# Nine more places for raw weights in the room of the attention pool, and fourth sums added by a transfer

## The chip, the core and the metric

The kernel runs on one core of one Trainium2 chip. The metric is the device time of one execution in microseconds (us). The core has five engines with instruction queues of their own: TensorE (PE, matmuls), VectorE (DVE), ScalarE (ACT), GpSimd (POOL) and SyncE (SP, which here only issues transfers). SP and POOL both issue DMA transfers, which run on the core's 16 DMA engines.

## What is computed

One decoder layer over 512 tokens of width 2048. The normalised input is multiplied by one wide weight matrix; eight heads of latent attention (MLA) and eight heads of forgetting attention (FoX) follow, each gated by a SiLU path, then one output projection, a norm and the residual sum.

```python
h = _rms_norm(x, g_pre)
proj = h @ w_in
(q_lat, kv_lat, k_rope_raw, gate_mla,
 fq, fk, fv, f_logit, gate_fox) = jnp.split(proj, split_points, axis=-1)
o_mla = _mla_branch(q_lat, kv_lat, k_rope_raw, g_q, w_uq, g_kv, w_ukv, cos, sin) * jax.nn.silu(gate_mla)
o_fox = _fox_branch(fq, fk, fv, f_logit, b_forget) * jax.nn.silu(gate_fox)
o = jnp.concatenate([o_mla, o_fox], axis=-1) @ w_out
return x + _rms_norm(o, g_post)
```

All inputs are float32. The kernel keeps that precision by writing every factor as a sum of a rounded high part and a remainder, and by three matmuls in place of one (`mm3`, lines 138 to 140: high x high, high x low, low x high).

## The kernel before, in words

**Chunks.** All weights come as chunks of 128 partitions x 1024 float32 (512 KB). `load` (lines 215 to 238) has SP fetch a chunk into a place of the tag "raw"; `divide` (240 to 251) has ScalarE cast it to its high part `whi` (L249) and VectorE subtract to get the low part `wlo` (L250). `chunk(i)` (line 260) is called when TensorE's program comes to chunk i: it loads up to chunk i+4, divides up to chunk i+2, and hands out the parts of chunk i. There are three raw places, three `whi` and three `wlo`, all in the pool `wp`. A place is free again when both parts of the chunk that had it are made, so SP, whose queue is in order, waits at a load until that place is free.

**Stages.** First the FoX heads in four pairs (projections fq, fk, fv, fg, interleaved with the attention of the pair before). Then the stage of the change, which runs from about 436 us to 603 us: two groups of columns of the input projection, "l" (the latents) and "m" (the MLA gates), each as a 2 x 2 block product done with seven half-block products in place of eight. Their names are p1, p2, p4, q6, g5, g7 and g3, each of four chunks. They run in the order p1 l, p1 m, p2 l, p2 m, p4 l, p4 m, then q6, g5, g7, g3 for l, and the same four for m. In the chunk numbers of the program, p1 l has raw73 to raw76, p1 m 77 to 80, p2 81 to 88, p4 l 89 to 92, p4 m 93 to 96, and q6 l begins with raw97. A last stage does the MLA heads (projections mq, mk, mv, interleaved with attention) and the output projection, which is made of half-block products too.

**Sums of weights.** Half-block products need sums of weight blocks. These are made ahead in DRAM, in steps (`add_step`, line 289): a plain copy of one block into a scratch tensor, and then an accumulating transfer from POOL that adds the second block. A step is issued after every so many half chunks (`set_pace`, `paced`), and begins with a 64-byte transfer from `whi` that ties it to TensorE's progress (the rows `t<-whi`). During the stage of the change the pace is 1000, so no step is issued; it is 2 during the MLA heads. The fourth sums (t4, used by p4) of l and m are left for late: p4's chunk is t6 loaded into a raw place, and a second block loaded beside it (`second`), which VectorE adds into the raw place (line 246) before the cast.

**Operands.** The sums of input blocks, which are the other factor, were put away in DRAM by POOL (`awaymg`), and are fetched back by SP in 256 KB pieces (`fetch`, line 908: bmq for q6, bmg for g5, g7 and g3) and divided by ScalarE and VectorE (lines 129 and 130). POOL puts away parts of the finished FoX heads in the first part of the stage in the same way (`awayoa`, `awayog`, line 884).

**Order.** Instructions of one engine run in the order of the program, which a scheduler sets from the order of the code and from its own estimates. Each transfer counts on one of eight counters of its queue in turn (DMAHW0 to 7 for SP, DMASW0 to 7 for POOL), and an issue waits for the one that had its counter before.

**Room.** The pool `pp` holds what the attention of the heads works with (probabilities, their parts, values). Before, it stays open from the start to the end of the heads, also during the stage of the change, in which it is not used.

Of the kernel before, what the change touches and what calls it, by code (L numbers as in the profile page):

```python
# [12 lines left out]
F32 = mybir.dt.float32  # L13
# [3 lines left out]
ALU = mybir.AluOpType  # L17
AX = mybir.AxisListType

P = 128  # L20
# [22 lines left out]
RND = 12582912.0  # L43
V3 = 3 * HW
NSLOT = 28


def split_const(c, bits, n):
# [15 lines left out]
def tile_hybrid_layer(  # L64
# [16 lines left out]
    nc = tc.nc  # L81
    pe, act, dve, pool = nc.tensor, nc.scalar, nc.vector, nc.gpsimd
# [4 lines left out]

    inner = ctx.enter_context(ExitStack())
    tb = inner.enter_context(tc.tile_pool(name="tb", bufs=1))
    pp = inner.enter_context(tc.tile_pool(name="pp", bufs=2))  # L90
    tp = inner.enter_context(tc.tile_pool(name="tp", bufs=4))
    dr = ctx.enter_context(tc.tile_pool(name="dr", bufs=1, space=bass.MemoryType.DRAM))
    ps = ctx.enter_context(tc.tile_pool(name="ps", bufs=4, space=bass.MemoryType.PSUM))

    def slot(name, dt=F32, shape=(P, 2, S)):

        return sp.tile(list(shape), dt, tag="s", name=name)
# [4 lines left out]
    def proj_bank(name):  # L102
        return bank("pj", name, 4)
# [90 lines left out]
    chunks = []  # L194
# [11 lines left out]

    raws, ready = {}, {}

    more = []

    def raw_tile(i):
        pool = more[0] if more and (i - more[1]) % 6 < 3 else wp
        return pool.tile([P, 1024], F32, tag="raw", name=f"raw{i}", bufs=3)

    def load(i, small=None):

        w, cols, k, n, width = chunks[i]
        if cols is None:

            raw = raw_tile(i)  # L220
            nc.sync.dma_start(raw, w)
            raws[i] = raw
            if k is not None:
                second = slot(f"second{i}")
                nc.sync.dma_start(second, k)
                raws[i] = raw, second.rearrange("p k c -> p (k c)")
            return
        if i < 2:
            raw = slot(f"raw{i}", shape=(P, 1024))
        else:  # L230
            raw = raw_tile(i)
        v = raw[:, : n * width].rearrange("p (k c) -> p k c", k=n)
        for at, off, cnt in cols:
            (nc.sync if cnt >= P or small is None else small).dma_start(
                v[:, :, at : at + cnt],
                w[0, k * P : (k + n) * P, off : off + cnt].rearrange("(k p) c -> p k c", p=P),
            )
        raws[i] = raw

    def divide(i):  # L240
        w, cols, k, n, width = chunks[i]
        m = n * width
        raw = raws.pop(i)
        if isinstance(raw, tuple):
            raw, second = raw
            dve.tensor_tensor(out=raw, in0=raw, in1=second, op=ALU.add)
        hi = wp.tile([P, 1024], F32R, tag="whi", name=f"whi{i}")
        lo = wp.tile([P, 1024], F32R, tag="wlo", name=f"wlo{i}")
        act.copy(hi[:, :m], raw[:, :m])  # L249
        dve.tensor_tensor(out=lo[:, :m], in0=raw[:, :m], in1=hi[:, :m].bitcast(F32), op=ALU.subtract)  # L250
        ready[i] = [t[:, :m].rearrange("p (k c) -> p k c", k=n) for t in (hi, lo)]
# [6 lines left out]
            state["divided"] += 1  # L258

    def chunk(i, ahead_load=4, ahead=2):  # L260
        while state["loaded"] < min(len(chunks), i + ahead_load + 1):
            load(state["loaded"])
            state["loaded"] += 1
        prepare(i + ahead)
        return ready.pop(i)

    fox = []
    for p in range(4):
        c = {}
# [45 lines left out]
    prods = {}  # L315
# [165 lines left out]
    def set_pace(n):  # L481
        state.update(pace=n, tiles=0)
# [435 lines left out]
    def along(a, b):  # L918
        return [lambda x=x, y=y: (x(), y()) for x, y in zip(a, b)]
# [4 lines left out]
    def operand(n, of):  # L924
        def parts(kk, t):
            return [oper[n, of][kk // 2][:, x, kk % 2, t * P : (t + 1) * P] for x in range(2)]

        return parts
# [126 lines left out]
    for p in range(4):  # L1055
        c = fox[p]
# [152 lines left out]
    def sums_wide(n):  # L1209
        return lambda kk: [oper[n, "m"][kk // 2][:, x, kk % 2, :] for x in range(2)]  # L1210
# [30 lines left out]
    def gate(f, top, bottom):  # L1241

        if f % 2 == 0:
            o_of.append(slot(f"gm{f // 2}"))
        g = o_of[-1][:, f % 2, :]
        pt = att_bank(f"gmt{f}")
        c = slice(f % 4 * P, (f % 4 + 1) * P)
        for t in range(NT):
            pe.transpose(pt[:, t * P : (t + 1) * P], (top, bottom)[t // 2][:, t % 2, c], ident)
        act.activation(g, pt, AF.Tanh)  # L1250
        dve.scalar_tensor_tensor(out=g, in0=g, scalar=1.0, in1=pt, op0=ALU.add, op1=ALU.mult)
        gm.append(g)

    set_pace(1000)
    A, A2 = ([proj_bank(f"g{n}{t}") for t in range(2)] for n in "lm")
    product("p1", "l", x_wide(0, 0), A, True, True, turned=True)
# [22 lines left out]
    scaled(c21, B2, 2, pb)  # L1279
    drain()  # L1280
    C, G = ([proj_bank(f"g{n}l{t}") for t in range(2)] for n in "cd")
    product("q6", "l", sums_wide("q6"), C, True, True, side=[*f5[2:], *along(d5[:2], f7[:2])], turned=True)
    raws_of += [slot(f"lat{i}") for i in (2, 3)]
    lat_sum(lat_block(1, 0), C, pl, ALU.subtract)
# [34 lines left out]
    drain()  # L1319
    for f in range(4, 8):  # L1320
        todo.append(lambda f=f: gate(f, c12, c22))
    qnh, qnl = zip(*(latents[i] for i in range(6)))
    knh, knl = zip(*(latents[i] for i in range(6, 10)))


    for p in range(4):
        c = mla[p]
        if p == 3:
            for f in (*fetches("a11", "o"), *fetches("a12", "o")):
                f()  # L1330
        qb = [proj_bank(f"mq{p}{i}") for i in range(3)]

        proj_T(c["q"], [(qb[i], P, cols(i * P)) for i in range(3)], qnh, qnl, rate=2)
        q = [[split(qb[i], f"mq{p}{i}", SC_M, first=P)] for i in range(2)]
        wholes = slot(f"mw{p}")
        qw = [[whole_block(wholes, i, qb[i], SC_M)] for i in range(2)]
        a, b = rotate(qb[2], P, SC_M, f"q{p}")
        for i in range(2):
            r = tmp(f"rq{p}{i}")
            src = slice(ROPE * i, ROPE * (i + 1))  # L1340
            for half in range(2):
                dve.tensor_tensor(
                    out=r[ROPE * half : ROPE * (half + 1), :], in0=a[src, :], in1=b[src, :], op=ALU.add
                )
            q[i].append(split(r, f"rq{p}{i}", first=P))
            qw[i].append(whole_block(wholes, 4 + i, r))
        if p == 0:
            set_pace(2)
        if p == 3:
            todo.extendleft([*divisions("a11", "o"), *divisions("a12", "o")])  # L1350
        kb = [proj_bank(f"mk{p}{i}") for i in range(2)]
        vb = [proj_bank(f"mv{p}{i}") for i in range(2)]

        def v_cols(w, j):
            return w[:, j, :].rearrange("p (h c) -> p h c", h=2)[:, :, NOPE:]

        kk = 0
        for i in c["kv"]:
            hi, lo = chunk(i)
            for j in range(chunks[i][3]):  # L1360
                fst, lst = kk == 0, kk == KVR // P - 1
                for n in range(2):
                    w = cols(256 * n)
                    mm3(kb[n], w(hi, j), w(lo, j), knh[kk], knl[kk], fst, lst)
                for t in range(NT):
                    o = vb[t // 2][:, (t % 2) * 256 : (t % 2) * 256 + 256]
                    ts = slice(t * P, (t + 1) * P)
                    mm3(
                        o, knh[kk][:, ts], knl[kk][:, ts], v_cols(hi, j), v_cols(lo, j),
                        fst and t % 2 == 0, lst, skip_group_check=True,  # L1370
                    )
                kk += 1
                pump(2)
                behind(hi)
        k = [[split(kb[i], f"mk{p}{i}"), (kr, None)] for i in range(2)]
        kw = [[whole_block(wholes, 2 + i, kb[i]), kr.bitcast(F32)[:, :P]] for i in range(2)]
        drain()
        values_into(v_pair(f"mv{p}"), slice(0, 256), [piece_of(vb, t, 256)[0] for t in range(NT)])
        vs = values_of(f"mv{p}")
        heads = [  # L1380
            Head(
                f"m{2 * p + i}", q[i], k[i],
                vs[i],
                lambda h=2 * p + i: gm[h],
                list(zip(qw[i], kw[i])),
            )
            for i in range(2)
        ]
        enqueue_scores(heads)
        enqueue_values(heads)  # L1390
        done += heads
# [124 lines left out]
            s()  # L1516

    product("p2", 0, operand("a12", "o"), A, False, True, 2, (6, heads_end))
    inner.close()
    op = ctx.enter_context(tc.tile_pool(name="op", bufs=8, reuse_waits="tile"))  # L1520
    more.extend([op, state["loaded"]])
# [9 lines left out]
    f = og_of[1, 0]  # L1531
# [78 lines left out]
```

## Time and profile before

| | before |
|---|---|
| median of three runs | 910.28 us (908.63 to 911.88) |
| the profiled execution | 912.14 us, span 910.4 us |
| TensorE busy | 898.7 us, 99% of the span |
| VectorE busy | 625.2 us, 69% |
| ScalarE busy | 424.6 us, 47% |
| granted TensorE clock | 0.997 of full speed |
| moved by DMA | 199.40 MB, mean 219 GB/s |

The span runs from the first to the last instruction; the rest of the execution lies around it. A row of the timeline gives the start, the duration, engine, line, operation, what is written and read, and in brackets the idle time of the engine just before with what ended it. A matmul's end is modelled, and matmuls overlap, so how long one step of TensorE takes is read from one start to the next. A row of the waits gives who waited for whom: us in total, times, the longest. A row of the windows gives the stretch, its length, the busy time of each engine with its number of instructions, the granted clock, the mean share of the DMA engines that were busy, and GB/s.

### The profile page before, as it was taken

To read this page: it belongs to the slowest core of one execution; us is meant where nothing else is said; L and a number is where in the kernel's file an instruction comes from. 1 tells how busy PE (TensorE), PEld (TensorE's weight loads), DVE (VectorE), ACT (ScalarE), POOL (GpSimd) and SP (SyncE) were. 2 spreads that over 40 slices of the span, in tenths; PEclk is the share of its full clock that TensorE was granted. 3 is DMA by queue.
4 is the path that set the end of the run, shared out by engine and by line. 5 is a ranking of instruction groups with operands and counts; after the bars stand their busy time and mean duration, and the time that the engine had idled before them with its cause. 6 is when DMAs were issued, how large, how long until landed. Compare 5 with 4: busy or idle time off the path is not lost.

```text
span 910.4 us, 12934 instructions
## 1 busy us (share of the span) xinstructions
PE 898.7 (99%) x4732; PEld 774.3 (85%) x4732; DVE 625.2 (69%) x1074; ACT 424.6 (47%) x779; POOL 80.9 (9%) x97
## 2 busy tenths in 40 slices
PE   8999999999999999999999999999999999999997
PEld 8988888898889988888998998878888888888885
DVE  3467778537563684474758777978877986886585
ACT  5773333234222342242464556644554565654483
POOL 1010110110120110111100000001101000000021
PEclk9999999999999999999999999999999999999998
DMA  9378987987898798899798875559999546786878
GB/s 291 96 197 192 250 218 199 231 222 195 231 256 210 200 233 226 228 219 228 228 312 304 289 221 162 162 157 230 215 231 254 117 122 203 243 257 216 278 188 251
DMA packets 121364, 199.40 MB, mean 219 GB/s; under 512 B 16050, under 2 KB 59596, under 8 KB 121300
## 3 DMA queue, kind: packets, MB, share of 16 engines
q1 hardware_dynamic: 105044, 158.84, 55.5%
q0 software_dynamic: 15520, 39.33, 23.5%
q8 instruction: 37, 0.61, 0.3%
q10 hardware_dynamic: 736, 0.40, 0.2%
q14 instruction: 27, 0.22, 0.1%
HBM read 186.46 MB, written 70.80 MB: 283 GB/s over the span
## 4 chain that ended last, share of the span: by engine, by line
PE 92%; DVE 4%; DMA 2%; ACT 1%; issue 1%; SPq 0%; ACTq 0%; DVEq 0%
PE fv L561 4%; PE fg L138 3%; PE fq L140 3%; PE fq L138 3%; PE fq L139 3%; PE fg L140 3%; PE fg L139 3%; PE fk L139 3%; PE fk L140 3%; PE fk L138 3%; PE sm L604 3%; PE fv L140 2%; PE fv L138 2%; PE fv L139 2%; PE mq L138 2%; PE mq L140 2%
## 5 line engine op out<-in xcount | busy, mean ns | idle before, releaser
L250 DVE TENSOR_TENSOR wlo<-raw,whi 128x1024 fp32r<-128x1024 f32 (+3 forms) x205 | 242.8, 1186 | 172.3 <-ACT whi L249 162.2
L249 ACT CAST whi<-raw 128x1024 fp32r<-128x1024 f32 (+3 forms) x205 | 209.4, 1022 | 297.5 <-PE fk L139 52.9
L138 PE MATMUL fq<-h,whi 128*128 128x512 f32 x128 | 52.6, 411 | 0.0
L138 PE MATMUL fg<-h,whi 128*128 128x512 f32 x128 | 51.0, 398 | 0.0
L140 PE MATMUL fq<-h,wlo 128*128 128x512 f32 x128 | 50.3, 393 | 0.0
L139 PE MATMUL fq<-h,whi 128*128 128x512 f32 x128 | 50.1, 391 | 0.0
L140 PE MATMUL fg<-h,wlo 128*128 128x512 f32 x128 | 50.1, 391 | 0.0
L138 PE MATMUL fk<-h,whi 128*128 128x512 f32 x128 | 50.0, 391 | 0.0
L139 PE MATMUL fg<-h,whi 128*128 128x512 f32 x128 | 49.9, 390 | 0.0
L139 PE MATMUL fk<-h,whi 128*128 128x512 f32 x128 | 49.8, 389 | 0.0
L140 PE MATMUL fk<-h,wlo 128*128 128x512 f32 x128 | 49.8, 389 | 0.0
L294 POOL DMA_DIRECT2D t<-in_w_out_dram x16 | 18.5, 1159 | 261.8 <-DMA t<-in_w_out_dram 232.1
L140 PE MATMUL fv<-whi,h 128*128 128x256 f32 (+1 forms) x128 | 39.5, 309 | 0.0
L139 PE MATMUL fv<-wlo,h 128*128 128x256 f32 (+1 forms) x128 | 39.5, 309 | 0.0
L138 PE MATMUL fv<-whi,h 128*128 128x256 f32 (+1 forms) x128 | 39.5, 309 | 0.0
L561 PE MATMUL fv<-whi,h 128*128 128x456 f32 x128 | 38.9, 389 | 0.0
L621 ACT ACTIVATE pf<-sf,stf 128x128 f32<-128x128 f32 (+3 forms) x32 | 16.9, 528 | 26.9 <-DVE stf L619 26.9
L138 PE MATMUL mq<-ln,whi 128*128 128x512 f32 x72 | 28.8, 400 | 0.0
L140 PEld LDWEIGHTS fq<-h,wlo 128*128 128x128 f32 x128 | 24.0, 188 | 5.4
L140 PEld LDWEIGHTS fg<-h,wlo 128*128 128x128 f32 x128 | 24.0, 188 | 5.3
L139 PE MATMUL mq<-ln,whi 128*128 128x512 f32 x72 | 28.3, 393 | 0.0
L140 PEld LDWEIGHTS fk<-h,wlo 128*128 128x128 f32 x128 | 24.0, 188 | 5.0
(525 smaller groups left out, 2456.8 us busy)
## 6 DMA issues: line engine op xcount, KB each, us to landing
raw<-in_w_in_dram SPq DMA_DIRECT2D x80, 512.0 KB
t<-in_w_out_dram SPq DMA_DIRECT2D x32, 512.0 KB
raw<-t SPq DMA_DIRECT2D x32, 512.0 KB
raw<-in_w_out_dram SPq DMA_DIRECT2D x24, 512.0 KB
t<-in_w_out_dram POOLq DMA_DIRECT2D x16, 512.0 KB, 8.5
t<-t POOLq DMA_DIRECT2D x16, 512.0 KB, 7.5
awaymg<-rmg POOLq DMA_DIRECT2D x8, 512.0 KB, 8.6
raw<-t6l SPq DMA_DIRECT2D x8, 512.0 KB
```

Source lines behind the costliest of these rows:

```text
L138: pe.matmul(o, ah, bh, start=first, stop=False, **kw)
L139: pe.matmul(o, ah, bl, start=False, stop=False, **kw)
L140: pe.matmul(o, al, bh, start=False, stop=last, **kw)
L249: act.copy(hi[:, :m], raw[:, :m])
L250: dve.tensor_tensor(out=lo[:, :m], in0=raw[:, :m], in1=hi[:, :m].bitcast(F32), op=ALU.subtract)
L294: pool.dma_start(to.rearrange("p (k c) -> p k c", k=2), second, accum_op=ALU.add)
L561: pe.matmul(banks[t][:, :n], a[k][:, tss[t]], b[:, j, :], start=k == 0 and m == 0, stop=k == NK - 1 and m == 2,)
L604: pe.matmul(s[:, :nn], a[:, qs], c[:, :nn], start=(i == 0), stop=(i == len(pairs) - 1))
L621: act.activation(p, s[:, :n], AF.Exp, bias=st[:, 0:1], accum_out=st[:, 1:2])
```

## The change

Three things change. The pool `pp` is closed before the stage and opened again after it; in its room a pool `rw` holds nine more raw places, so that of every twelve chunks of the stage nine go to `rw` and three to `wp`. `chunk` then loads further ahead, one chunk more for every two, up to twelve ahead. The fourth sums are added by an accumulating transfer from POOL into the raw place that holds t6; the loads of `second` and VectorE's adds go. Beside that, `add_step` has a pace of 10 from q6 l on (1000 before) and of 3 from the first pair of MLA heads on (2 before).

```diff
+DEEP = 9
...
-    pp = inner.enter_context(tc.tile_pool(name="pp", bufs=2))
     tp = inner.enter_context(tc.tile_pool(name="tp", bufs=4))
+    heads_room = ctx.enter_context(ExitStack())
+    pp = heads_room.enter_context(tc.tile_pool(name="pp", bufs=2))
...
-    more = []
+    more, deep = [], []
 
     def raw_tile(i):
+        if deep and deep[1] <= i < deep[2] and (i - deep[1]) % (DEEP + 3) < DEEP:
+            return deep[0].tile([P, 1024], F32, tag="raw", name=f"raw{i}", bufs=DEEP)
         pool = more[0] if more and (i - more[1]) % 6 < 3 else wp
         return pool.tile([P, 1024], F32, tag="raw", name=f"raw{i}", bufs=3)
...
             nc.sync.dma_start(raw, w)
+            if k is not None:
+                pool.dma_start(raw.rearrange("p (k c) -> p k c", k=2), k, accum_op=ALU.add)
             raws[i] = raw
-            if k is not None:
-                second = slot(f"second{i}")
-                nc.sync.dma_start(second, k)
-                raws[i] = raw, second.rearrange("p k c -> p (k c)")
             return
...
         raw = raws.pop(i)
-        if isinstance(raw, tuple):
-            raw, second = raw
-            dve.tensor_tensor(out=raw, in0=raw, in1=second, op=ALU.add)
...
     def chunk(i, ahead_load=4, ahead=2):
-        while state["loaded"] < min(len(chunks), i + ahead_load + 1):
+        upto = i + ahead_load
+        if deep:
+            upto = max(upto, min(i + DEEP + 3, deep[2] - 1, state["loaded"] + i % 2))
+        while state["loaded"] < min(len(chunks), upto + 1):
...
+    heads_room.close()
+    room = ctx.enter_context(ExitStack())
+    deep.extend(
+        [
+            room.enter_context(tc.tile_pool(name="rw", bufs=DEEP, reuse_waits="tile")),
+            state["loaded"], prods["g3", "m"][-1] + 1,
+        ]
+    )
     set_pace(1000)
...
     C, G = ([proj_bank(f"g{n}l{t}") for t in range(2)] for n in "cd")
+    set_pace(10)
     product("q6", "l", ...)
...
+    deep.clear()
+    room.close()
+    pp = heads_room.enter_context(tc.tile_pool(name="pp", bufs=2, reuse_waits="tile"))
...
         if p == 0:
-            set_pace(2)
+            set_pace(3)
```

The first place is SP's queue at the start of the stage, where the first nine places of `rw` are filled. Before:

```order
L234 DMA raw76_3916<-in_w_in_dram 128x2x512 [waits DMAHW7_49,DVE_49]
L234 DMA raw77_3975<-in_w_in_dram 128x2x512 [waits DMAHW2_49,DMAHW0_49,DVE_49]
L234 DMA raw78_4007<-in_w_in_dram 128x2x512 [waits DMAHW5_49,DVE_49]
L234 DMA raw79_4041<-in_w_in_dram 128x2x512 [waits DMAHW7_49,DVE_49]
L234 DMA raw80_4076<-in_w_in_dram 128x2x512 [waits DMAHW3_49,DMAHW0_49,DVE_49]
```

And now:

```order
L236 DMA raw76_3916<-in_w_in_dram 128x2x512 [waits DMAHW7_49,DVE_49]
L236 DMA raw86_4166<-in_w_in_dram 128x2x512 [waits DMAHW2_49,DMAHW0_49,DVE_49]
L236 DMA raw77_3979<-in_w_in_dram 128x2x512 [waits PE_49]
L236 DMA raw78_3981<-in_w_in_dram 128x2x512 [waits PE_49]
L236 DMA raw79_4013<-in_w_in_dram 128x2x512 [waits DMAHW3_49,PE_49,Activation_49]
L236 DMA raw80_4047<-in_w_in_dram 128x2x512
```

Before, each load waits for VectorE, which frees the place of an earlier chunk. Now raw77 to raw85 wait for TensorE's last use of the heads' values (PE) or for nothing but their counter, and raw86, which goes to `wp`, stands ahead of them.

The second place is SP's queue ahead of the fourth products. Names: raw89 to raw96 are the chunks of p4, bmq and bmg the fetched operands. Before:

```order
L908 DMA bmq60_4246<-awaymg50_2270 128x512 [waits DMASW4_49]
L908 DMA bmq61_4278<-awaymg51_2471 128x512 [waits DMASW7_49,DMASW4_49,PE_49]
L908 DMA bmq62_4310<-awaymg52_2657 128x512 [waits DMASW0_49,PE_49]
L908 DMA bmq63_4342<-awaymg53_2936 128x512 [waits PE_49]
L234 DMA raw86_4248<-in_w_in_dram 128x2x512 [waits DMAHW6_49,DVE_49]
L234 DMA raw87_4280<-in_w_in_dram 128x2x512 [waits DMAHW7_49,DVE_49]
L234 DMA raw88_4312<-in_w_in_dram 128x2x512 [waits DMAHW0_49,DVE_49]
L221 DMA raw89_4348<-t6l0_109 128x1024 [waits DMAHW5_49,DMASW2_49,DVE_49]
L225 DMA second89_4350<-in_w_in_dram 128x2x512 [waits DMAHW1_49,DMASW3_49,DMASW2_49]
L908 DMA bmg50_4368<-awaymg50_2270 128x512 [waits DMAHW2_49,PE_49]
L221 DMA raw90_4370<-t6l1_110 128x1024 [waits DMAHW6_49,DMAHW3_49,DVE_49]
```

And now:

```order
L225 DMA raw92_4297<-t6l3_112 128x1024 [waits DMAHW7_49,DMASW3_49,DVE_49]
L910 DMA bmq60_4262<-awaymg50_2270 128x512 [waits DMAHW0_49,DMASW4_49]
L910 DMA bmq61_4295<-awaymg51_2471 128x512 [waits DMAHW1_49,DMASW7_49,DMASW4_49]
L225 DMA raw93_4300<-t6m0_125 128x1024 [waits DMAHW2_49,DMASW0_49,DVE_49]
L910 DMA bmq62_4331<-awaymg52_2657 128x512 [waits DMAHW3_49,DMASW0_49]
L225 DMA raw94_4333<-t6m1_126 128x1024 [waits DMAHW4_49,DMASW3_49,DVE_49]
L910 DMA bmq63_4364<-awaymg53_2936 128x512 [waits DMAHW5_49,PE_49]
L225 DMA raw95_4370<-t6m2_127 128x1024 [waits DMAHW6_49,DVE_49]
L225 DMA raw96_4373<-t6m3_128 128x1024 [waits DMAHW7_49,DVE_49]
L225 DMA raw97_4394<-t6l0_109 128x1024 [waits DMAHW0_49,DVE_49]
L910 DMA bmg50_4392<-awaymg50_2270 128x512 [waits DMAHW1_49,DMASW3_49,DMASW2_49]
L910 DMA bmg51_4412<-awaymg51_2471 128x512 [waits DMAHW2_49,PE_49]
```

The fetches bmq stood ahead of raw86 and stand behind raw92 now; bmg50 stood between raw89 and raw90 and stands behind raw97 now, with bmg51. Almost every row waits for a counter, that is, for the transfer eight before it.

The third place is VectorE at the end of p2 m and the start of p4 l. Before:

```order
L250 TENSOR_TENSOR wlo88_4375<-raw88_4312,whi88_4374 128x1024
L246 TENSOR_TENSOR raw89_4348<-raw89_4348,second89_4350 128x1024
L130 TENSOR_TENSOR bmg50_4368<-bmg50_4368 128x512
L250 TENSOR_TENSOR wlo89_4398<-raw89_4348,whi89_4397 128x1024
L246 TENSOR_TENSOR raw90_4370<-raw90_4370,second90_4372 128x1024
L130 TENSOR_TENSOR bmg51_4390<-bmg51_4390 128x512
L250 TENSOR_TENSOR wlo90_4419<-raw90_4370,whi90_4418 128x1024
```

And now:

```order
L249 TENSOR_TENSOR wlo88_4397<-raw88_4191,whi88_4396 128x1024
L132 TENSOR_TENSOR bmg50_4392<-bmg50_4392 128x512
L132 TENSOR_TENSOR bmg51_4412<-bmg51_4412 128x512
L249 TENSOR_TENSOR wlo89_4419<-raw89_4220,whi89_4418 128x1024
L249 TENSOR_TENSOR wlo90_4437<-raw90_4223,whi90_4436 128x1024
```

The adds (L246) are gone, and the second half of bmg51 stands ahead of wlo89 where it stood ahead of wlo90; ScalarE has its casts of the two in the same places.

More of the change, by code (lines that the diff above doesn't have):

```diff
@@ L1518, in tile_hybrid_layer @@
     product("p2", 0, operand("a12", "o"), A, False, True, 2, (6, heads_end))
+    heads_room.close()
     inner.close()
```

## The prediction

> **What bounds the kernel now.** I read the page first, then the list of waits on TensorE, then the order of time around the one wait that the change touches.
>
> ```profile
> span 910.4 us, 12934 instructions
> PE 898.7 (99%) x4732; PEld 774.3 (85%) x4732; DVE 625.2 (69%) x1074; ACT 424.6 (47%) x779; POOL 80.9 (9%) x97
> ...
> PE gbm L139 <- DVE wlo L250: 1.1, 2, 0.6
> ...
> PE sm L604 <- ACT pm L621: 1.0, 1, 1.0
> PE gdm L139 <- DVE wlo L250: 0.7, 1, 0.7
> ```
>
> TensorE is busy for 99% of the span, so the time changes only where it stops. Of its waits inside the kernel, three lie where the change works: in the fourth product of the second group (gbm), in the heads (sm) and in the last product of the stage (gdm). Matmuls overlap, so the true loss is read from start to start. Here is TensorE in time around gbm:
>
> ```profile
> 492.65 0.63 PE L138 MATMUL gbm<-whi,h 128*128 128x512 f32 x2
> 493.28 0.50 PE L139 MATMUL gbm<-wlo,h 128*128 128x512 f32 x1
> 493.62 0.39 PE L140 MATMUL gbm<-whi,h 128*128 128x512 f32 x1
> 493.85 0.39 PE L139 MATMUL gbm<-wlo,h 128*128 128x512 f32 x1
> ...
> 495.69 0.63 PE L138 MATMUL gbm<-whi,h 128*128 128x512 f32 x2
> 496.83 0.50 PE L139 MATMUL gbm<-wlo,h 128*128 128x512 f32 x1 [0.52 <-DVE wlo L250]
> ...
> 499.24 0.63 PE L138 MATMUL gbm<-whi,h 128*128 128x512 f32 x2
> 500.47 0.50 PE L139 MATMUL gbm<-wlo,h 128*128 128x512 f32 x1 [0.61 <-DVE wlo L250]
> ```
>
> One step is 0.23 us (493.62 to 493.85), so two take 0.46. The three pairs took 0.63, 1.14 and 1.23, which is 0.17 + 0.68 + 0.77 lost, and the step after each took 0.34 instead of 0.23 (493.28 to 493.62), 0.11 more: 1.62 + 0.33 = 1.95, call it 2.0 us. Why it waits there stands in ScalarE and VectorE just before:
>
> ```profile
> 487.37 1.05 ACT L249 CAST whi<-raw 128x1024 fp32r<-128x1024 f32 x1 [2.50 <-DVE raw L246]
> 490.92 1.05 ACT L249 CAST whi<-raw 128x1024 fp32r<-128x1024 f32 x1 [2.50 <-DVE raw L246]
> ...
> 488.45 1.23 DVE L250 TENSOR_TENSOR wlo<-raw,whi 128x1024 fp32r<-128x1024 f32 x1 [1.19 <-ACT whi L249]
> 489.59 1.22 DVE L246 TENSOR_TENSOR raw<-raw,second 128x1024 f32<-128x1024 f32 x1
> ```
>
> Add, cast and subtract form a ring: 490.92 − 487.37 = 3.55 us a chunk, while TensorE eats one in 12 x 0.23 = 2.76 us. Over eight chunks the ring falls behind by more than the two chunks prepared ahead. It is not short of data: the ring ends in VectorE.
>
> **What a transfer costs.** The windows give transfer rates: columns after the clock are the share of the 16 DMA engines and GB/s.
>
> ```profile
> 470.00:500.00 30.00, 29.35 (x174) 25.16 (x172) 22.11 (x22) 13.26 (x16) 0.00 (x0) 1.00 0.91 321
> 474.00:478.00 4.00, 4.00 (x20) 3.30 (x19) 3.14 (x4) 1.91 (x3) 0.00 (x0) 1.00 1.04 394
> 886.00:890.00 4.00, 4.00 (x19) 3.33 (x18) 2.42 (x3) 2.90 (x4) 2.66 (x3) 1.00 1.13 208
> 657.00:667.00 10.00, 9.97 (x63) 8.72 (x62) 6.97 (x15) 5.07 (x14) 1.17 (x1) 1.00 1.00 246
> 500.00:620.00 120.00, 118.87 (x730) 105.90 (x731) 96.38 (x142) 65.85 (x93) 1.20 (x1) 1.00 0.65 197
> 620.00:710.00 90.00, 88.92 (x510) 77.38 (x508) 73.39 (x157) 46.19 (x115) 12.89 (x13) 1.00 0.95 230
> ...
> q0 software_dynamic: 15520, 39.33, 23.5%
> ...
> t<-in_w_out_dram POOLq DMA_DIRECT2D x16, 512.0 KB, 8.5
> ...
> 879.77 2.71 POOL L1427 DMA_DIRECT2D c<-in_x_dram  x3 [165.06 <-ACT c L1426]
> ```
>
> Plain loads alone fill the engines at 394 GB/s: 512 KB (524 kB) takes 1.33 us. Accumulating transfers into SBUF alone (886 to 890, those issued from 879.77 on) run at 208 GB/s: 2.52 us. Queue q0 as a whole, mostly accumulates, took 0.235 x 910.4 = 214 us for 39.33 MB, 2.85 us per 512 KB. I take 2.85, since the new accumulates run among loads, as most of q0 does. From issue to landing one takes 8.5 us. Both kinds together (657 to 667) move 246 GB/s, 2.13 us per 512 KB, about the mean of 1.33 and 2.85: they share the engines, and neither gives way. So 470 to 500, at 0.91 today, has little room.
>
> The Trainium skill, "DMA: Bandwidth & Descriptors", section on the anatomy of a DMA issued from GpSimd, fits 2.0 us plus bytes over 436 GB/s: 1.2 us of data movement and 3.2 us to landing here. By it the five accumulates below would cost 6.0 us and not 14.3. The rows of accumulates in this trace (208 GB/s, 8.5 us) contradict it.
>
> **The change, part by part.** *The adds leave VectorE.* Eight adds of 1.22 us go, the ring is cast and subtract alone (1.05 + 1.23 us, under 2.76), and the 2.0 us stall goes: **−2.0**.
>
> *The loads run ahead.* The "degrees" order only the program. SP issues a load as soon as its place is free, and the nine places come free with the fox heads' last products:
>
> ```profile
> 431.63 0.37 SPq L234 DMA_DIRECT2D raw<-in_w_in_dram  x1
> ...
> 440.26 7.46 SPq L234 DMA_DIRECT2D raw<-in_w_in_dram  x4
> ...
> 437.50 0.71 POOL L884 DMA_DIRECT2D awayoa<-gf  x1 [10.32 <-DVE gf L652]
> ...
> awayog<-rog POOLq DMA_DIRECT2D x4, 512.0 KB, 4.4
> ...
> 470.97 0.42 SPq L908 DMA_DIRECT2D bmg<-awaymg  x1
> ...
> 475.74 0.62 ACT L129 CAST bmg<-bmg 128x512 fp32r<-128x512 f32 x1 [1.50 <-DMA bmg<-awaymg]
> ...
> 481.14 0.28 PE L138 MATMUL gbl<-h,whi 128*128 128x256 f32 x1
> ```
>
> Before, SP issued nothing between 431.63 and 440.26. After, I let the burst start at 435. From there on the engines have no gap, and what matters is what stands behind in the queue. In the order of the changed program the fetches bmg50 and bmg51, issued 4.8 us ahead of their cast today (470.97 to 475.74), stand behind raw97, and ScalarE and VectorE have both of them ahead of chunk raw89, the first of the fourth product. So raw89 cannot be converted before bmg51 is in. Ahead of that landing lie:
> - 21 loads (raw86, 77 to 85, 87 to 97) x 1.33 = 27.9 us;
> - six fetches of 256 KB (four bmq, two bmg) x 0.67 = 4.0;
> - the puts of POOL, one of 256 and four of 512 KB, at the price of loads: 6.0;
> - accumulates: eight exist; the first load to be added to is the 13th (13 x 1.33 + 6.0 puts = 23 us, 458), data can move some 4 us later, and from there each of the last loads and fetches shares with one. I take five: 14.3.
>
> The sum is 52.2 us: bmg51 lands at 487.2. Its cast (0.62), raw89's cast (1.05) and 0.2 of hand-over put the fourth product's first matmul at 489.1 instead of 481.14: **+8.0**. Part of it may show as waits in the product before, for the bmq fetches are late alike. Bounds: accumulates at 2.52 and four ahead: 48.0 us, +3.8; all eight ahead: 60.8 us, +16.6; none sharing: 37.9 us, landing at 473, 0.
>
> *The sums after that.* The last accumulate has behind 435 four more loads, all puts and eight accumulates: 25 x 1.33 + 4.0 + 6.0 + 22.8 = 66 us, 501. Its chunk is used at 500.9 without a stall (492.65 + 3 x 2.76), so cast by 498.6 at the latest (1.05 + 1.23 ahead), and by 506.6 with one of 8.0. It hides behind the first wait: 0; without that cover it would cost 2.4.
>
> *The steps of the output weights' sums.* The pace of 10 puts seven steps (64 + 6 half chunks) into 500 to 612, the pace of 3 leaves eleven instead of seventeen for the heads. A step moves a copy and an accumulate, 2 x 2.13 = 4.3 us; seven are 30 us, and 500 to 620 has 0.35 x 120 = 42 us free: 0, with loads twelve ahead as cover. Without it each step would hold SP for the landing of its mark:
>
> ```profile
> SPq L297 <- DMA t<-whi: 59.8, 24, 6.0
> ...
> 693.39 0.82 SPq L908 DMA_DIRECT2D boa<-awayoa  x2
> ...
> 700.02 0.62 ACT L129 CAST boa<-boa 128x512 fp32r<-128x512 f32 x1 [1.28 <-DMA boa<-awayoa]
> ...
> 615.41 1.20 POOL L294 DMA_DIRECT2D t<-in_w_out_dram  x1 [162.77 <-DMA t<-in_w_out_dram]
> ```
>
> 59.8/24 = 2.5 us each, 17 in all. In the heads the load falls from 0.95, and the sm wait goes, since it came from the boa fetch that took 6.6 us (693.39 to 700.02): **−1.0**; bounds 0 and −1.4, with the score matmuls around it.
>
> *With one answer.* POOL's new waits hold nothing: its queue was empty for 162.77 us before 615.41. The heads' pool reopens in a room that the last deep chunk has left some 30 us before: 0. The gdm wait stays, VectorE being full there: 0.
>
> **Sum:** −2.0 + 8.0 − 1.0 = +5.0 us. The profiled execution took 912.14 us (span 910.4 and 1.7 around it) and would take 917.1. The median of the runs shown is 910.28, 1.9 lower; the forecast for it is **915.3 us**.
>
> **Rivals.**
> 1. *The transfers keep up.* If the backlog is below 44.2 us (435 to 479.2, the latest landing without a stall, 481.14 less the 1.9 of casts and hand-over), the 2.0 and 1.0 are pure gain: 907.3. For it: accumulates share only once their own load is in, and POOL's issue of 8.5 us may keep them off the engines until bmg51 has passed. Against it: 37.9 us are there without any, which leaves room for two, and 657 to 667 shows no yielding. Chance 0.18.
> 2. *An accumulate moves like a load*, at 1.33 us (row 474 to 478): 37.9 + 6.7 = 44.6 us, landing at 479.6, 0.4 late: +0.4 − 3.0 = −2.6, 907.7, just within the bound below. The page's fit above, which would make this so, is the only ground for it. Chance 0.04.
> 3. *A draw.* Four accumulates ahead at 2.52 and a burst that starts 1 us earlier: +2.8 − 3.0, 910.1. Chance 0.10.
> 4. *All eight accumulates go ahead of the fetch.* 60.8 us, +16.6 − 3.0: 923.9. For it: POOL can issue them 1.2 us apart (the 1.20 of the row at 615.41) once their loads are in. Against it: the last loads stand just ahead of the fetch. Chance 0.08.
> 5. The forecast has 0.60; its own range runs from 913.5 (five accumulates at 2.52: 50.5 us, +6.2 − 3.0) to 918.1 (six at 2.85: 55.0 us, +10.8 − 3.0).
>
> That the places stay unused is no case: they need nothing but the heads' products, done before the stage.
>
> **Numbers.** Below 0.3%, 2.7 us, a measurement of this kernel hardly tells a change from none. Faster: rival 1, 0.18. Same: rivals 2 and 3, 0.14. Slower: 0.68. The range runs from 907, rival 1, to 922, above the forecast's own end and short of rival 4 alone.
>
> **What would show it.** Right: ScalarE waits once for DMA bmg for over 5 us just ahead of the fourth product; TensorE waits 5 to 10 us there, on whi or wlo; no wait at gbm by the ring; a DMA share of about 1.0 from 440 to 500; accumulates landing over 10 us after issue; no sm wait. Wrong: bmg landing within 9 us of its issue, or the fourth product starting on time.

## The result and the profile after

The changed kernel took 917.82 us (median of four runs, 917.04 to 920.07), the kernel before beside it 909.61. The ratio is 1.0091, 95% interval [1.0063, 1.0118]: slower by about 8.3 us. The profiled execution took 917.16 us, and its span is 915.4. The experiments ran in three sets, each on one chip, so every verdict below is such a ratio to runs of the kernel before on the same chip.

The page, after:

```profile
span 915.4 us, 12938 instructions
PE 898.2 (98%) x4732; PEld 774.8 (85%) x4732; DVE 617.3 (67%) x1066; ACT 423.9 (46%) x779; POOL 90.1 (10%) x105
```

TensorE's waits (total us, times, longest):

```profile
PE gbl L140 <- ACT whi L248: 4.9, 1, 4.9
PE mix L1466 <- ACT scaler L1465: 1.9, 1, 1.9
...
PE gcl L142 <- DVE wlo L249: 0.8, 1, 0.8
PE gm L141 <- DVE wlo L249: 0.8, 1, 0.8
PE gdm L141 <- DVE wlo L249: 0.7, 1, 0.7
PE gm L140 <- ACT whi L248: 0.5, 1, 0.5
PE gbl L142 <- DVE wlo L249: 0.5, 1, 0.5
```

The gbm wait of before is gone, and one of 4.9 us stands ahead of the fourth product (gbl). The gm rows are the end of the second product, the gcl row is one of the l products after p4. What ScalarE did ahead of it:

```profile
482.56 0.62 ACT L131 CAST bmg<-bmg 128x512 fp32r<-128x512 f32 x1 [6.69 <-DMA bmg<-awaymg]
484.51 0.62 ACT L131 CAST bmg<-bmg 128x512 fp32r<-128x512 f32 x1 [1.33 <-DMA bmg<-awaymg]
485.03 1.99 ACT L248 CAST whi<-raw 128x1024 fp32r<-128x1024 f32 x2
```

ScalarE stands for 6.7 us before bmg50, then for bmg51, which is in at 484.5. Only then comes the cast of raw89. TensorE in time:

```profile
480.86 0.39 PE L142 MATMUL gm<-whi,h 128*128 128x512 f32 x1
486.12 0.58 PE L140 MATMUL gbl<-h,whi 128*128 128x256 f32 x1 [4.88 <-ACT whi L248]
...
487.38 0.58 PE L142 MATMUL gbl<-h,wlo 128*128 128x256 f32 x1 [0.46 <-DVE wlo L249]
...
490.11 0.41 PE L142 MATMUL gbl<-h,wlo 128*128 128x256 f32 x1
490.33 0.36 PE L140 MATMUL gbl<-h,whi 128*128 128x256 f32 x1
...
490.52 0.28 PE L141 MATMUL gbl<-h,whi 128*128 128x256 f32 x1
490.64 0.28 PE L142 MATMUL gbl<-h,wlo 128*128 128x256 f32 x1
```

The matmuls behind the wait start 0.22 us apart (490.11 to 490.33) and then 0.12 (490.52 to 490.64). The windows name the reason (granted clock, DMA share and GB/s stand last):

```profile
430.00:440.00 10.00, 10.00 (x70) 9.21 (x70) 6.02 (x9) 4.31 (x7) 1.82 (x3) 1.00 0.99 297
...
478.00:482.00 4.00, 3.24 (x15) 2.35 (x13) 0.00 (x0) 0.00 (x0) 1.20 (x1) 1.00 1.09 287
482.00:486.00 4.00, 0.00 (x0) 0.00 (x0) 1.38 (x2) 2.11 (x4) 0.00 (x0) 0.71 1.08 294
486.00:490.00 4.00, 3.41 (x14) 3.12 (x15) 3.21 (x3) 3.12 (x5) 0.00 (x0) 0.50 1.11 246
490.00:494.00 4.00, 4.00 (x33) 4.00 (x33) 1.60 (x2) 1.05 (x1) 0.00 (x0) 0.94 1.09 287
```

While TensorE stood idle its granted clock fell, and it was 0.50 for the first 4 us of p4 l. The DMA engines were full throughout (1.08 to 1.11), and had been from 430 on (0.99).

Since both kernels run the same matmuls, the start of each can be set against its start in the trace of before. The change of that offset over a part of the program is what the part gained or lost. In us, each trace against that of before (ahead: up to the first matmul of p1 l; the numbered rows are the experiments):

```
                       ahead   p1,p2   wait for   in     in    q6 l to  m prod-  heads
                               products  p4 l    p4 l   p4 m    g3 l     ucts
changed kernel         -1.87    1.81     5.05    2.48  -2.04    1.02    -0.01   -1.60
1 no accumulates       -1.99    0.00     0.00    0.00  -2.04    0.70    -0.04   -1.61
2 second loads         -1.90    0.00     0.00    0.00  -2.04    0.00    -0.02   -0.98
3 fetches earlier       0.21    0.00     0.00    1.49   4.76    1.83    -0.05   -1.60
4 old paces            -2.33    3.54     5.01    3.12  -2.04    0.00     0.00    0.60
5 accumulates p4 m     -2.08    0.00     0.00    0.00  -2.04    2.38     0.01   -1.61
6 accumulates p4 l     -2.98    9.79     0.00    0.00  -2.04    0.16     0.09   -1.60
7 busy wait, 42        -0.68    1.80     9.31    0.08  -2.04    0.55    -0.06   -1.60
8 places alone         -2.34    0.00     0.00    0.00  -2.04    0.00    -0.06   -1.55
9 busy wait, 21        -1.88    3.10     5.09    1.12  -2.04    0.24     0.00   -1.62
10 loads by GpSimd     -1.56   12.00     0.00    0.00  -2.04    0.67    -0.04   -1.61
11 new paces alone     -2.16    0.00     0.00    0.00   1.83    2.44     4.62   -1.59
12 accumulate alone    -2.40    0.00     3.75    9.82   4.02   -0.01    -0.01   -1.53
```

In the changed kernel the stage of the half-block products lost 1.81 + 5.05 + 2.48 − 2.04 + 1.02 − 0.01 = 8.3 us, what the ratio says if neither the first nor the last column is an effect of the change. The first is none: nothing is changed ahead of the stage, and eleven of these thirteen traces stand 1.5 to 3 us ahead there, so that the profiled run of before was a late one. The last column is taken up with the paces below. A row is one execution, and rows and ratios agree only to some 3 us: by its ratio experiment 2 lies 5.3 us below before, by its row 2.06 in the stage and 0.98 in the heads. The runs of before beside it went from 909.22 to 917.43 us. So the list tells where time was lost, and the ratio how much in all.

### The profile page after: what moved, and what is told of

Its sections match the earlier page's. It is cut to its first block, busy times and chain, and to the rows that moved or that the text cites. A ratio compares the mean times of both kernels' runs of the same rounds, so it can differ in the third digit from the quotient of the medians.

```text
span 915.4 us, 12938 instructions
## 1 busy us (share of the span) xinstructions
PE 898.2 (98%) x4732; PEld 774.8 (85%) x4732; DVE 617.3 (67%) x1066; ACT 423.9 (46%) x779; POOL 90.1 (10%) x105
## 5 line engine op out<-in xcount | busy, mean ns | idle before, releaser
L296 POOL DMA_DIRECT2D t<-t x16 | 13.3, 829 | 162.6 <-DMA t<-in_w_out_dram 129.3
```

Of the source, the lines that this page charges most:

```text
L296: pool.dma_start(to.rearrange("p (k c) -> p k c", k=2), second, accum_op=ALU.add)
```

## Experiments

Theory A is the prediction's: the work that stands ahead of bmg51 on the DMA engines, with accumulates at 2.85 us, delays it. Theory B puts the delay down to the place of the fetch behind 21 loads, theory C to a cost of accumulates wherever they stand, theory D to GpSimd's queue.

**1. The accumulates left out.**

```diff
-            if k is not None:
-                pool.dma_start(raw.rearrange("p (k c) -> p k c", k=2), k, accum_op=ALU.add)
```

> The changed kernel without its eight accumulating transfers (p4 is then computed from the sums t6 alone, b21 is left out). Theory A (backlog: each accumulate takes the engines about 2.85 us, and that work ahead of bmg51 makes it late): the queue ahead of bmg51 is 37.9 us from 433, it lands by about 472, the waits in p2 m (1.8 us), at the start of p4 l (5.0) and the slow clock behind it (2.5 with the wait on wlo) all go: 9.3 us less than the changed kernel, about 907 to 909. Theory B (place in the queue: the 21 loads ahead of the fetch are enough by themselves): ScalarE still waits over 4 us for bmg and the time stays at 914 to 918.

This kernel leaves the second block out of p4's weights, so it tells of time only. 907.35 us, ratio 0.9945 [0.9925, 0.9965]. The three losses around p4 l are 0.00 in the list above. B falls: with the same 21 loads ahead of it, the fetch came in time.

**2. Second loads and adds in place of the accumulates**, places and paces as changed.

```diff
-                pool.dma_start(raw.rearrange("p (k c) -> p k c", k=2), k, accum_op=ALU.add)
+                second = slot(f"second{i}")
+                nc.sync.dma_start(second, k)
+                raws[i] = raw, second.rearrange("p k c -> p (k c)")
+                return
...
+        if isinstance(raw, tuple):
+            raw, second = raw
+            dve.tensor_tensor(out=raw, in0=raw, in1=second, op=ALU.add)
```

> The changed kernel with its nine places and its paces, but the fourth sums made as before: a second load by SP and an add on VectorE for each of the eight chunks. Theory A: eight plain loads of 1.33 us stand where accumulates of 2.85 stood; with five of them ahead of bmg51 the queue is 37.9 + 6.7 = 44.6 us from 433, it lands at about 478, in time; the adds are back in the ring, but data that lie ready early let it start early, so between 0 and 2.0 us of the gbm wait come back: 906 to 910. Theory B: more loads than ever stand ahead of the fetch, the wait at p4 l stays at 4 us or more: 914 to 920.

906.92 us, ratio 0.9942 [0.9918, 0.9965]: below both kernels, and by medians (of different sets of runs) 10.9 below the changed one. The same bytes are read. The DMA view gives the price of each form; first the changed kernel from 475 to 500 us, q0 being GpSimd's queue (accumulates only) and q1 SP's:

```profile
q0 software_dynamic: 1493, 2.87, 62.1%
q1 hardware_dynamic: 1315, 4.30, 46.3%
```

0.621 x 25 us = 15.5 us for 2.87 MB is 2.83 us per 512 KB; q1 has 0.463 x 25 for 4.30 MB, 1.41 us. In experiment 2, 462 to 477 us, second loads among the others:

```profile
q1 hardware_dynamic: 2596, 5.90, 103.9%
```

1.039 x 15 us for 5.90 MB is 1.39 us per 512 KB: half the price. And the adds cost nothing. VectorE of experiment 2 at the last add, and in p4 m, which began 1.90 us earlier than before, at 490.75:

```profile
480.52 1.23 DVE L257 TENSOR_TENSOR wlo<-raw,whi 128x1024 fp32r<-128x1024 f32 x1 [0.35 <-ACT whi L256]
481.67 1.22 DVE L253 TENSOR_TENSOR raw<-raw,second 128x1024 f32<-128x1024 f32 x1
...
491.91 1.23 DVE L257 TENSOR_TENSOR wlo<-raw,whi 128x1024 fp32r<-128x1024 f32 x1 [0.27 <-ACT whi L256]
494.79 1.23 DVE L257 TENSOR_TENSOR wlo<-raw,whi 128x1024 fp32r<-128x1024 f32 x1 [1.65 <-ACT whi L256]
```

With nine places more, all eight adds are over by 483 us (481.67 + 1.22), before p4 m begins. The ring of add, cast and subtract is not there in p4 m, and the −2.04 is the same as with accumulates.

**3. Fetches one product earlier.**

```diff
-    product("p1", "m", x_block(0, 0), A2, True, True)
+    f6 = fetches("q6", "m")
+    f5, f7, f3 = (fetches(n, "m") for n in ("g5", "g7", "g3"))
+    product("p1", "m", x_block(0, 0), A2, True, True, side=f6)
...
-    product("p2", "l", ..., side=fetches("q6", "m"), turned=True)
+    product("p2", "l", ..., side=f5[:2], turned=True)
...
-    product("p2", "m", ..., side=f5[:2])
+    product("p2", "m", ...)
```

> The changed kernel with the fetches bmq issued along p1 m and bmg50, bmg51 along p2 l, one product earlier each; loads and accumulates are the same. Theory A: the wait for bmg ahead of p4 l goes, but the engines have the same work up to the last accumulate (503 in the changed kernel), and its chunk is wanted by 499: 1 to 5 us of wait move into p4 m (gbm); 910 to 915. Theory B (only the place in the queue counts): all of the wait goes, 907 to 909.

916.16 us, ratio 1.0044 [1.0025, 1.0063]. The wait ahead of p4 l is gone and 1.49 + 4.76 us stand in p4 itself (in an execution of 918.79 us, 2.6 above the median). There ScalarE waits for the accumulates, one after another:

```profile
484.11 1.05 ACT L248 CAST whi<-raw 128x1024 fp32r<-128x1024 f32 x1 [1.87 <-DMA raw<-in_w_in_dram]
489.27 1.05 ACT L248 CAST whi<-raw 128x1024 fp32r<-128x1024 f32 x1 [4.12 <-DMA raw<-in_w_in_dram]
494.28 1.04 ACT L248 CAST whi<-raw 128x1024 fp32r<-128x1024 f32 x1 [3.96 <-DMA raw<-in_w_in_dram]
498.95 1.05 ACT L248 CAST whi<-raw 128x1024 fp32r<-128x1024 f32 x1 [3.63 <-DMA raw<-in_w_in_dram]
```

They arrive 4.9 us apart (484.11 to 498.95, three steps), where TensorE uses one in 2.76. The engines' time, not the place of the fetch, was short. That is theory A, a little above its range.

**4. The old paces.**

```diff
-    set_pace(10)
...
-            set_pace(3)
+            set_pace(2)
```

> The changed kernel with the paces of before (none in the half-block products, 2 in the heads). The wait of 4.9 us ahead of p4 l stays to within 1 us in both theories, since no step of the output weights lies before 500 in either. If the pace of 3 is what took the sm wait (1.5 us by start times) away, it is back between 700 and 715; if the steps at pace 10 are what delayed a bmg fetch to 9.0 us and gave gcl its loss of 1.0, that one goes. Net +0.5: 917 to 920. If the sm wait does not come back: 915 to 917.

919.44 us, ratio 1.0081 [1.0052, 1.0110], not to be told from the changed kernel. TensorE's waits:

```profile
PE gbl L140 <- ACT whi L248: 4.8, 1, 4.8
...
PE sm L606 <- ACT pm L623: 1.7, 1, 1.7
```

The wait ahead of p4 l stays, the 1.02 of the products from q6 l on is 0.00, and the sm wait is back. What delayed gcl, and with it the 1.02 us, in the changed kernel stands in its GpSimd and ScalarE:

```profile
526.28 1.15 POOL L296 DMA_DIRECT2D t<-in_w_out_dram  x1 [46.80 <-DMA t<-in_w_out_dram]
...
537.25 1.29 ACT L131 CAST bmg<-bmg 128x512 fp32r<-128x512 f32 x2 [4.95 <-DMA bmg<-awaymg]
```

ScalarE waits for a bmg fetch again, 4.95 us, behind a step of the output weights (526.28). Experiment 4, which has no such step, loses nothing there; experiment 2, which has it, does not either, so the step alone does not settle it.

**5 and 6. Half of the accumulates**: for p4 m only, then for p4 l only; the other four chunks as in experiment 2.

```diff
+                if i in prods["p4", "l"]:   # experiment 6: prods["p4", "m"]
+                    second = slot(f"second{i}")
+                    nc.sync.dma_start(second, k)
+                    raws[i] = raw, second.rearrange("p k c -> p (k c)")
+                    return
```

> The changed kernel with second loads and adds for the four chunks of p4 l, and accumulates only for the four of p4 m. Theory A (the accumulates' time on the engines): those four have 10 us more until they are wanted, so nothing waits and the time is that of the second loads for all, 905 to 909. Theory C (an accumulate in this queue costs SP or ScalarE something whatever its place, e.g. a wait of SP behind it that holds up the fetches): half of the loss of the changed kernel against the second loads (10.9 us) is left, 911 to 914.

> The other half: accumulates for p4 l, second loads and adds for p4 m. Theory A: in the changed kernel four accumulates landed before bmg51 and four behind it. Here four are ahead again, with up to four second loads among them (1.33 us each), so the waits ahead of and in p4 l stay at 4 to 8 us and the time is 913 to 918, although the count of accumulates is that of the other half. Theory C: as the other half, 911 to 914.

Late half 908.67 us, 0.9971 [0.9957, 0.9985]; early half 916.23, 1.0057 [1.0037, 1.0076]. The same number of accumulates, and 7.6 us apart: C falls. In the early half the loss stands in p2 m (9.79), where ScalarE waits for the bmq fetches, which are behind the same transfers:

```profile
ACT bmq L131 <- DMA bmq<-awaymg: 14.6, 3, 6.3
```

So the size was expected, its place not. The late half lost 2.38 us after q6 l, to bmg fetches beside a step issued at 518.82.

**7 and 9. The wait filled with idle matmuls**, 42 and then 21.

```diff
+    w2 = att_bank("warm2")
+    for i in range(42):   # experiment 9: 21
+        pe.matmul(w2[:, :P], warm, warm, start=True, stop=True)
     product("p4", "l", ...)
```

> The changed kernel with 42 matmuls of 128x128 on zeros (0.11 us each, 4.6 us) on TensorE between p2 m and p4 l, where it stood idle for 4.9 us. If the first 4 us of p4 l ran at half pace because the wait had lowered the granted clock (0.50 there), the clock stays at 1.00, 2.0 us are won and the time falls to 915 to 916.5. If they were slow by transfers or by late data, the time stays at 917 to 919 or grows by what the 42 take beyond the wait.

> The busy wait again, with 21 such matmuls: in the run with 42 each left two records of 0.11 us, 9.5 us in all and 4.3 us beyond the wait, so 21 should take 4.7 us and end just before the data are in. If the low clock (0.50 granted) after the wait is what slowed the first 4 us of p4 l, its matmuls run at 0.12 us from the first on and the time is 1.5 to 2.5 us below the changed kernel's 917.8: 915 to 916.5. If not: 917 to 919.

With 42: 919.23 us, 1.0083 [1.0063, 1.0103]. They took twice the time that I had set down (9.54 us), 4.3 beyond the wait, but p4 l lost 0.08 us instead of 2.48. With 21: 916.76, 1.0055 [1.0037, 1.0074], against 1.0091 for the changed kernel; the intervals overlap, so the total alone does not decide. TensorE and the clock of experiment 9 do, in its timeline and its window behind the wait:

```profile
482.37 4.85 PE L1287 MATMUL warm<-warm 128*128 128x128 f32 x42
487.45 0.38 PE L140 MATMUL gbl<-h,whi 128*128 128x256 f32 x1 [0.23 <-ACT whi L248]
...
488.71 0.38 PE L142 MATMUL gbl<-h,wlo 128*128 128x256 f32 x1 [0.76 <-DVE wlo L249]
...
489.17 0.28 PE L142 MATMUL gbl<-h,wlo 128*128 128x256 f32 x1
489.29 0.28 PE L140 MATMUL gbl<-h,whi 128*128 128x256 f32 x1
```

```profile
486.00:490.00 4.00, 3.01 (x23) 2.61 (x23) 3.05 (x3) 4.00 (x6) 0.00 (x0) 1.00 1.08 290
```

The 21 matmuls left 42 records, two each. With TensorE kept busy the clock stays at 1.00 and the matmuls stand 0.12 us apart as soon as wlo is there (489.17 to 489.29), beside the same transfers (1.08). The 1.12 us that p4 l still lost are mostly that wait for wlo (0.76 in the row of 488.71). The 2.0 us were the clock.

**8. The places alone**: experiment 2 with the old paces (its diff and that of experiment 4 together).

> The nine places alone: second loads and adds for all eight, and the paces of before. If the gbm stall (2.0 us) goes because the data are there early and the adds run ahead of the ring, and the sm wait (1.0 to 1.5) goes only with the pace of 3, this is 1 to 1.6 us above the kernel with second loads and new paces (906.9): 907.9 to 908.5, still 1.5 to 2.5 below before. If the paces did most of it: 909 to 911.

909.06 us, 0.9981 [0.9964, 0.9998]. The gbm stall is gone (−2.04) without any change to pace or adds. No sm wait shows either, against what I expected; but the profiled execution, 906.52 us, is the fastest of twelve and 2.5 below the median, so it need not stand for the others.

**10. The second loads issued by GpSimd.**

```diff
-                    nc.sync.dma_start(second, k)
+                    pool.dma_start(second, k)
```

> The kernel with second loads and adds, but the eight second loads are issued by GpSimd on its queue, where the accumulates stood. Same issuer and bytes as the accumulates, without the addition in the transfer. Theory A (the addition in the transfer is what costs engine time): they move at the price of loads, at most 2 us of wait comes back from their being later in the queue; 906.5 to 909.5. Theory D (GpSimd's queue is the slow part, added or not): landings 4 to 5 us apart as for the accumulates, a wait at p4 l of over 4 us, 913 to 919.

918.69 us, 1.0073 [1.0050, 1.0096]: the number of theory D, but not by its mechanism. The queues from 462 to 477 us, and then GpSimd and ScalarE in time:

```profile
q0 software_dynamic: 940, 3.45, 59.8%
q1 hardware_dynamic: 938, 2.43, 42.9%
```

```profile
451.08 4.29 POOL L229 DMA_DIRECT2D second<-in_w_in_dram  x6
...
475.96 0.62 ACT L131 CAST bmq<-bmq 128x512 fp32r<-128x512 f32 x1 [14.80 <-DMA bmq<-awaymg]
```

0.598 x 15 us for 3.45 MB is 1.36 us per 512 KB, the price of a plain load, so GpSimd's queue is not slow. But it takes 0.6 of the engines. Six of its loads are issued from 451.08 on, for a product that began at 481.14 before, and SP's queue with the bmq fetch has 0.429 of the engines beside them: 12.00 us are lost in p2 m. My 2 us left out that a second queue is served beside SP's, not behind it.

**11. The new paces alone**: the kernel before with `set_pace(10)` ahead of q6 l and `set_pace(3)` in the heads.

> The kernel before with the new paces (10 from q6 l on, 3 in the heads) and nothing else. If the pace of 3 takes the sm wait away and the steps at pace 10 are hidden, 1.0 to 1.5 below before: 908.5 to 910 beside 909.6 to 911.4. If the steps delay loads that are only 4 ahead here, waits of 1 to 4 us come up between 500 and 600 and it is 910 to 914.

917.13 us, 1.0060 [1.0039, 1.0081]. With loads only four ahead the steps cost 2.44 us in the products up to g3 l and 4.62 in those after; 1.7 of the 4.62 stand at the first projection of the MLA heads. The 1.83 in p4 m stand ahead of the first step. There VectorE's last add waited for its second load, on top of the ring:

```profile
497.74 1.23 DVE L246 TENSOR_TENSOR raw<-raw,second 128x1024 f32<-128x1024 f32 x1 [1.36 <-DMA second<-in_w_in_dram]
```

Why that load was late stays open. With the nine places the same steps cost 0.00 to 2.4.

**12. The accumulate alone**: the kernel before with the accumulates, without the places and with the old paces.

> The kernel before with the accumulates into the raw place in place of the second loads and adds, without the nine places and with the old paces. A place is free to be loaded only three chunks ahead (some 8 us of matmuls), and load and accumulate together take 4 + 8.5 us to land, so p4 must wait for each round of three places: several waits of 2 to 5 us in p4, 8 to 18 us in all, 918 to 928. If an accumulate were as cheap as a load, 910 to 914.

927.02 us, 1.0171 [1.0141, 1.0201]. TensorE in p4 waits once for each round of places:

```profile
482.49 0.39 PE L138 MATMUL gbl<-h,whi 128*128 128x256 f32 x1 [3.59 <-ACT whi L247]
...
498.33 0.38 PE L138 MATMUL gbl<-h,whi 128*128 128x256 f32 x1 [3.34 <-ACT whi L247]
...
512.85 0.51 PE L138 MATMUL gbm<-whi,h 128*128 128x512 f32 x1 [3.42 <-ACT whi L247]
```

With the slow starts behind them that makes 3.75 + 9.82 + 4.02 = 17.6 us. Without the places, both the new paces (experiment 11) and the accumulate make the kernel slower.

## Why the prediction was right

**The fetch behind the burst** (+8.0) was the right mechanism. The queue was to take 52.2 us from 435 and bmg51 to land at 487.2. SP issued raw77, the first load of the nine places, 2.1 us earlier than that, and the engines were full from then on (0.99 from 430 to 440):

```profile
432.91 1.39 SPq L236 DMA_DIRECT2D raw<-in_w_in_dram  x3
```

bmg51 was in at 484.5, 2.7 us ahead of the forecast; from 432.91 on that is 51.6 us, against 52.2 by the sum. An accumulate cost 2.83 us, as set down (2.85). From landing to first matmul went 486.12 − 484.51 = 1.6 us (1.9 forecast). The delay is 1.81 in p2 m, where the late bmq fetches show as the prediction said they might, and 5.05 ahead of p4 l, 6.9 in all.

**The clock** was not in the sum, which took TensorE to lose time only where it stops: +2.0, and beside it 0.5 of a late wlo. The Trainium skill, "TensorE: Matmul & The Clock Gate", Part 1, on the clock gate, says that an idle window of about 3.4 us halves the clock until a busy window has passed; the trace agrees, with 4.9 us idle, 0.50 granted, and half pace from 486.12 to 490.33.

**The adds leave VectorE** (−2.0): the size is exact (−2.04), the reason was too narrow. "It is not short of data" fails: in experiments 2 and 8 the adds stay and the stall goes, since early data let the adds run before the ring is pressed for time. The accumulate was not needed for it: with it the stage took 8.3 us more than before, with second loads in the same places 2.06 less.

**The pace** (−1.0 for sm) is not shown. Among the old paces, the trace of before and experiment 4 have the wait and experiments 8 and 12 have none; with the pace of 3, experiment 2 still has 0.4 us of it. The heads are 1.5 to 1.6 us shorter than in the trace of before in nearly all traces, whatever the pace. Experiment 2 is 0.39% below experiment 8, but their intervals meet. Whether the pace of 3 gains anything stays open.

**The steps** at 0 were a little wrong. Loads twelve ahead do cover most of them, as experiment 11 shows, which has the steps without the places and loses 2.44 + 4.62 us. But the bmg fetches are not among these loads, and one of them cost 1.02 us.

**The rivals.** That the transfers keep up is excluded by the wait at bmg. That an accumulate moves like a load is excluded by 2.83 against 1.41 us. From issue to landing the eight accumulates of the stage took 21.4 us in the median:

```profile
raw<-in_w_in_dram POOLq DMA_DIRECT2D x8, 512.0 KB, 21.4
```

The fit in the Trainium skill, "DMA: Bandwidth & Descriptors", section "Anatomy of one DMA — SWDGE (gpsimd) path", gives 3.2 us for a transfer of this size; the trace does not agree for an accumulate in a full queue. That all eight go ahead of the fetch is excluded too. The last three were issued from 470.71 on and took at least 22.5 us to land, which is behind 484.5:

```profile
470.71 1.20 POOL L227 DMA_DIRECT2D raw<-in_w_in_dram  x1 [3.57 <-DVE wlo L249]
...
DMA to landing us min/median/max: 22.5/22.8/25.0
```

**The total** of +5.0 was meant for the stage and the heads; the stage alone measured 8.3. The forecast of 915.3 is 2.5 low. Four terms were missing or counted wrongly: the clock (2.0), the fetch beside a step (1.0), the sm gain counted to the change (1.0) and the late wlo (0.5). Two things go the other way: a wait forecast 1.1 too long, and a median of before that now stands 0.7 lower. 2.0 + 1.0 + 1.0 + 0.5 − 1.1 − 0.7 = 2.7, which leaves 0.2 to the spread of the runs. That 917.82 still falls into the forecast's own range (913.5 to 918.1) is partly luck, since the errors offset one another. It is wholly luck that the profiled execution, 917.16 us, meets the 917.1 of the sum: behind its 5.0 us stand 8.3 in the stage and, against them, the first and last columns of the list.

## What to carry to other kernels

Deeper prefetch is worth what its transfers leave to the rest of the queue: count, in microseconds of engine time, everything issued ahead of the next operand that has no prefetch of its own, and give that operand its place first. Replacing an add on a compute engine by an addition in the transfer doubled the DMA engines' time for that transfer here (2.83 us against 1.41); with the places already there the add could simply have run earlier. A wait of TensorE of several microseconds is to be counted with the slow clock behind it, here 2.0 us for 4.9.

## What I had not expected of the hardware

- A queue of GpSimd is served beside SP's, at 0.6 of the engines in both windows that were read, for plain loads (59.8%) and for accumulates (62.1%). So the same second loads cost 12 us when GpSimd issued them early, and nothing in SP's order. In experiment 10 the two queues moved 940 and 938 packets in the same 15 us: as if they took turns by the packet, so that the queue with the larger packets (3.45 MB against 2.43 MB) gets more; in the changed kernel the counts are further apart, 1493 and 1315. The Trainium skill, "DMA: Bandwidth & Descriptors", section "Queues, rings and completion order", states such a turn; the trace of experiment 10 agrees, and no priority of the queue that is wanted first shows.
- Added in the transfer, 512 KB in SBUF take 2.83 us of the engines beside loads of 1.41; two full queues then deliver an accumulate every 4.9 us.
- A wait of 4.9 us brought the granted clock to 0.50, and the first 4.2 us behind it ran at half pace; 4.85 us of idle matmuls in the same place kept it at 1.00.
